# Moving three modulation products of layer 0 from the long convolutions to the filter stage

## The chip, the cores and the metric

The kernel runs on one core of a Trainium2 chip, in one launch. The metric is the device time of that launch in microseconds (us). The core has five engines with queues of their own, each in order: TensorE (PE; its weight loads are shown as PEld), VectorE (DVE), ScalarE (ACT), GpSimd (POOL) and SyncE (SP). In this kernel POOL and SP do little but issue DMA transfers.

## The reference

Two layers of a hybrid block over 512 latent and 256 context tokens of width 1024, in float32. Each layer modulates its input, mixes tokens in four head groups, projects, and runs an MLP:

```python
mod = jax.nn.silu(c) @ w_mod[i] + b_mod[i]          # and mod_c from c_ctx
sh1, sc1, g1, sh2, sc2, g2 = jnp.split(mod[:, None, :], 6, axis=-1)
h = rms_norm(x, norm_mix_pre[i]) * (1.0 + sc1) + sh1
y = token_mixers(h, ...)       # SSD scan, Hyena long convolution, two attentions; then w_out
x = x + g1 * rms_norm(y, norm_mix_post[i])
h = rms_norm(x, norm_mlp_pre[i]) * (1.0 + sc2) + sh2
x = x + g2 * rms_norm(squared_relu_mlp(h, mlp_w1[i], mlp_w2[i]), norm_mlp_post[i])
```

The context tokens go the same way with `mod_c` (in layer 0 only to the end). `w_mod[i]` is 1024 x 6144, so each of the six pieces sh1 to g2 needs a 1024 x 1024 block of it, 4 MB, for two rows of input. The Hyena convolution needs a filter for each layer and sequence length, made by a small network and turned into spectra. The filters depend on weights alone, and the modulation on `c`, `c_ctx` and weights.

## The kernel before

Everything is written in one Python class that emits instructions; a tile framework then sets each engine's order with a scheduler of its own, from the order of the program, priorities and the pools. Weight products are made of three float32r matmuls each (high x high, high x low, low x high; lines 298 to 300).

**The beginning** (`run`). Filter spectra for layer 0's 512 tokens are woven with the first two modulation products (`mod_cols(0, 0, 0)` and `mod_cols(0, 1, 1)`). Then follow `pre_pair` (normalized, modulated and transposed input, tile `xl`/`xc`), the loads of the first two units of `w_in`, and the remaining filters by themselves: layer 1's for 512 tokens and layer 0's for 256 (`filter_seq`). Right after it `qkv_in(0, "d")` makes queries, keys and values of the dense attention; the scheduler lays its 288 matmuls (tile `pg`, 24 for each of six token tiles in q, 24 in kv) between those of the filters. Each filter piece ends in a tile `fk`, of which there is one buffer, written by DVE (lines 721, 722) and sent to the DRAM tensor `spec` by POOL (line 725). There are 12 such pieces after the weave. When the filters are done, their pools are released and attention takes the space.

**A modulation product** is `mod_section` (line 439). It has 8 steps; in each, SP loads a 512 KB piece of `w_mod` into a tile (line 447), and four matmuls of 2 x 256 outputs (line 449) add to four quarters of one PSUM bank. ACT copies the result out (line 457). `mod_cols` then turns the row into columns with 8 transposes (line 510) and a DVE operation or two; `mod_gate` adds `b_mod`, multiplies by a norm weight (line 528) and sends the rows to DRAM (line 530, tile `gated`). Outside the first weave the `w_mod` pieces go into the pool `raw` (tile `r`), three buffers, which the loads of `w_in`, `w_out` and the MLP weights use too (line 354).

**The stage of the long convolutions** (`layer`). After attention and the projections for Hyena and SSD, `weave` interleaves four generators: Hyena for 512 tokens, Hyena for 256 tokens, SSD, and the list `mods`. In layer 0 this list has four modulation products: the gate `g1`, the shift `sh2` and the scale `sc2` of layer 0, and the first of layer 1. Hyena fetches its transform tables (tile `ht`, by POOL) and its spectra (tiles `hf` and `t`, from `spec`, by SP at line 816). Then come `w_out` (tile `py`), the gated norm and the MLP. Layer 1 has the same stage without Hyena for 256 tokens, with four SSD tiles rather than six, and with no modulation product.

The fourth piece of `mod_list(0)`, the gate `g2`, is made in layer 0's MLP in both kernels.

Of the kernel before, what the change touches and what calls it, by code (L numbers as in the profile page):

```python
# [22 lines left out]
SEQ = 512  # L23
CTX = 256
# [141 lines left out]
ME = (4, 1, 2)  # L166
# [7 lines left out]
def chain(*gens):  # L174
    for g in gens:
        yield from g
# [7 lines left out]
class K:  # L184
# [471 lines left out]
    def filter_seq(self, l, n, tabs, v=""):  # L656
        self.mark("filter_seq")
        nc, A = self.nc, self.A
        self.st = "f"
        big = n == SEQ  # L660
        off = 0 if big else SEQ
        h = n // 2
        nj = 2 if big else 1
        nb = 2 * nj
        rl = slice(64 * l, 64 * l + 64)
        for o in range(2):
            ss = self.sm(4, F32, "ss")
            kds = []
            for c in range(2):
                kd = []  # L670
                dec = self.a("dec")[:, :n]
                with self.tc.high_priority(offset=PRIO_W):
                    nc.sync.dma_start(dec, A["decay"][c][:, off:off + n])
                for d in range(2):
                    p = self.a("pf1")[:, :n]
                    ch = 4 * o + 2 * d + c
                    nc.tensor.matmul(p, self.w3[rl, 128 * ch:128 * ch + 128], self.h2[rl, off:off + n], start=True, stop=True)
                    t = self.a("kd" + v)[:, :n]
                    nc.vector.scalar_tensor_tensor(t, p, self.pp[l][:, P_B3 + ch:P_B3 + ch + 1], dec, ADD, MUL)
                    nc.scalar.activation(p, t, AF.Square, accum_out=ss[:, 2 * d + c:2 * d + c + 1])  # L680
                    kd.append(t)
                    yield
                kds.append(kd)
            ms = self.sm(2, F32, "ms", 4)
            nc.vector.scalar_tensor_tensor(ms, ss[:, 0:2], EPS, ss[:, 2:4], ADD, ADD)
            r = self.rsqrt(ms, 2)
            yield
            for c in range(2):
                nc.vector.memset(kds[c][1][:, 0:1], 0.0)
                nc.scalar.activation(kds[c][1], kds[c][1], AF.Copy, scale=r[:, c:c + 1])  # L690
            for cs in range(2):
                X = [self.a("fx" + v, (nb, 256)) for _ in range(2)]
                for c in range(2):
                    kd = kds[c]
                    src = self.a("ko" + v)[:, :n]
                    nc.vector.scalar_tensor_tensor(src, kd[0], r[:, c:c + 1], kd[1], MUL, SUB if cs else ADD)
                    p = self.a("pf2")
                    for par in range(2):
                        for jc in range(nj):
                            s = src[:, 256 * jc + par:256 * jc + 256:2]  # L700
                            b = par * nj + jc
                            nc.tensor.transpose(p[:, 128 * b:128 * b + 128], s, self.ident)
                    pv = p[:, :128 * nb].rearrange("p (b c) -> p b c", c=128)
                    self.hi(X[0][:, :, 128 * c:128 * c + 128], pv)
                    self.lo(X[1][:, :, 128 * c:128 * c + 128], pv, X[0][:, :, 128 * c:128 * c + 128])
                    yield
                for kc in range(h // 128):
                    p = self.a("pmod" if not v and kc % 2 else "pf3")
                    for par in range(2):
                        for jc in range(nj):  # L710
                            b = par * nj + jc
                            if big:
                                th, tl = (tabs[2 * cs + par][:, jc, q, 128 * kc:128 * kc + 128] for q in range(2))
                            else:
                                th, tl = (tabs[0][:, cs, par, q, :] for q in range(2))
                            self.mm3(p[:, 256 * par:256 * par + 256], th, tl,
                                     X[0][:, b, :], X[1][:, b, :], jc == 0, jc == nj - 1)
                    od = self.t2((128, 256))
                    kt = self.a("fk" + v, (2, 256))
                    nc.scalar.activation(od, p[:, 256:512], AF.Copy)  # L720
                    nc.vector.tensor_tensor(kt[:, 0, :], p[:, 0:256], od, ADD)
                    nc.vector.tensor_tensor(kt[:, 1, :], p[:, 0:256], od, SUB)
                    for half in range(2):
                        dst = self.spec[l, n][kc + half * (h // 128)][:, 512 * cs + 256 * o:512 * cs + 256 * o + 256]
                        nc.gpsimd.dma_start(dst, kt[:, half, :])  # L725
                    yield
# [607 lines left out]
    def run(self):  # L1334
        nc = self.nc
        self.plan()
        self.setup()
        pf = self.push("fil", {"fh": (768, F32, 2), "fw": (256, F32, 1),
                               "kd": (512, F32, 4), "ko": (512, F32, 2),
                               "fk": (512, F32, 1), "fw3": (1024, F32, 1), "dec": (512, F32, 2),  # L1340
                               "ft": (1024, F32R, 4), "fx": (1024, F32R, 3)}, "right")
        pp = self.push("pp", {"pf1": (512, F32, 2), "pf2": (512, F32, 2), "pf3": (512, F32, 1),
                              "pmod": (512, F32, 1), "pg": (512, F32, 2)}, psum=True)
        fl = self.push("filL", {"kd0": (512, F32, 8), "ko0": (512, F32, 4), "fk0": (512, F32, 2), "fx0": (1024, F32R, 4), "wm": (1024, F32, 6)})
        self.filter_loads()
        tb = self.filter_tables(SEQ)
        self.filter_head()

        def pre(pair):
            self.mark("pre")  # L1350
            x2 = self.wsp_p.tile([128, 2, 4 * WU], F32, tag="w", name=self.nm("w"))
            xr2 = [x2[:, i, 0:1024] for i in range(2)]
            for i in range(2):
                nc.sync.dma_start(xr2[i], self.x_in(0, 2 * pair + i))
            self.pre_norm(xr2, xr2)
            return xr2
        xr = [pre(0)]
        self.weave((chain(self.mod_cols(0, 0, 0), self.mod_cols(0, 1, 1, P_NMIX)), W0[0]),
                   (self.filter_seq(0, SEQ, tb, "0"), W0[1]))
        self.pop(fl)  # L1360
        XTp = self.push_xt()
        fa = self.push("qkv", self.QKV_TAGS)
        XT = self.new_xt()
        xr += [pre(1), pre(2)]
        for pair in range(3):
            self.mark("pre")
            self.pre_pair(xr[pair], pair, XT, self.mods[0, 1], self.mods[0, 0], EN[0])
        self.load_units(1, 0)
        if self.nl > 1:
            self.do(self.filter_seq(1, SEQ, tb))  # L1370
        self.do(self.filter_seq(0, CTX, self.filter_tables(CTX)))
        self.setup2()
        self.qkv = self.qkv_in(0, "d", XT)
        self.pop(pp)
        self.pop(pf)
        for l in range(self.nl):
            XT, XTp, fa = self.layer(l, XT, XTp, fa)

    def layer(self, l, XT, XTp, fa):
        nc = self.nc  # L1380
# [3 lines left out]
        more = l + 1 < self.nl  # L1384
# [27 lines left out]
        YT = self.new_xt((0,), need)  # L1412
        self.load_units(self.upos[l, "o", 3])
        hys = [(self.hyena(l, SEQ, 0, YT), W2[0])]
        mods = self.mod_list(l)[0 if l == 0 else ME[0]:3 if l == 0 and more else 9]
        if need:
            hys.append((self.hyena(l, CTX, SEQ, YT), W2[3]))
        if l + 1 < self.nl:
# [215 lines left out]
```

## Time and profile before

| | before |
|---|---|
| median of 3 runs (range) | 1924.27 us (1921.92 to 1924.78) |
| the profiled execution | 1919.0 us |
| its span, first to last instruction | 1917.2 us |
| PE / DVE / ACT / POOL busy | 93% / 68% / 44% / 5% of the span |
| mean granted TensorE clock | 0.974 of full speed |
| chain that ended last, by engine | PE 76%, DVE 9%, issue 6%, DMA 4%, ACT 4% |
| DMA | 235 MB, mean 123 GB/s |

The profile shows one execution. Busy time of PE is modelled (matmuls are pipelined, and their ends are worked out), so a share of 95% does not mean that PE issues without a gap; the spacing of the starts tells that. The share of DMA is that of 16 engines; the clock is the mean that was granted, where 1.00 is 2.4 GHz.

### The profile page before, as it was taken

How to read it: one execution, taken by the hardware profiler on the slowest of the kernel's cores; microseconds unless marked ns; L12 is line 12 of the kernel's file. 1: busy time of each engine (PE TensorE's matmuls, PEld its weight loads, DVE VectorE, ACT ScalarE, POOL GpSimd, SP SyncE). 2: the span in 40 equal slices, each digit the busy share in tenths (PEclk: the TensorE clock that was granted, in tenths of full speed). 3: DMA queues.
4: the chain of work that ended last, by engine and by line, in shares of the span. 5: the costliest groups of instructions: out<-in, count | busy, mean ns of one | idle time of the engine just before them, and what ended most of it. 6: DMA issues, size and time to landing. Idle time of an engine off the chain costs nothing.

```text
span 1917.2 us, 27370 instructions
## 1 busy us (share of the span) xinstructions
PE 1790.2 (93%) x10170; PEld 1482.7 (77%) x10170; DVE 1297.7 (68%) x2897; ACT 836.8 (44%) x1804; POOL 91.5 (5%) x176
## 2 busy tenths in 40 slices
PE   6899999978879999999999998899978789999998
PEld 2688888845668888888888888888866688888886
DVE  4878888877756656676666658988878563444446
ACT  4844565536515532322222327556546263332322
POOL 0120001011000000000000000000010000000000
PEclk9999999989989999999999999999989899999999
DMA  8531121278833244333333415112183243233232
GB/s 291 187 111 53 39 74 58 69 260 272 290 107 132 93 135 136 121 107 114 121 121 121 142 47 176 45 48 89 45 273 120 74 157 113 91 99 99 88 102 85
DMA packets 137597, 235.16 MB, mean 123 GB/s; under 512 B 12466, under 2 KB 77395, under 8 KB 137464
## 3 DMA queue, kind: packets, MB, share of 16 engines
q1 hardware_dynamic: 122920, 186.12, 30.2%
q0 software_dynamic: 14544, 47.30, 7.1%
q8 instruction: 80, 1.31, 0.3%
q14 instruction: 53, 0.43, 0.1%
HBM read 206.74 MB, written 26.64 MB: 122 GB/s over the span
## 4 chain that ended last, share of the span: by engine, by line
PE 76%; DVE 9%; issue 6%; DMA 4%; ACT 4%; POOL 1%; SPq 0%; DVEq 0%; ACTq 0%; POOLq 0%
PE pg L298 19%; PE pg L299 18%; PE pg L300 18%; PE po L1294 3%; PE py L298 2%; PE py L299 2%; PE pm L1286 2%; PE py L300 2%; PE ps L1249 1%; PE ps L1250 1%; PE pm L1206 1%; PE psd L1052 1%; DMA spec<-fk 1%; POOL spec L725 1%; DMA r<-in_w_mod_dram 1%
## 5 line engine op out<-in xcount | busy, mean ns | idle before, releaser
L265 ACT ACTIVATE w<-r 128x1024 fp32r<-128x1024 f32 (+1 forms) x176 | 186.6, 1061 | 348.1 <-PE pg L300 325.1
L270 DVE TENSOR_TENSOR w<-r,w 128x1024 fp32r<-128x1024 f32 (+1 forms) x176 | 214.1, 1223 | 106.1 <-ACT w L265 105.2
L298 PE MATMUL pg<-xl,w 128*128 128x512 f32 (+1 forms) x704 | 269.5, 386 | 2.2 <-DVE ya L1311 0.9
L300 PE MATMUL pg<-xl,w 128*128 128x512 f32 (+1 forms) x704 | 269.7, 384 | 0.0
L299 PE MATMUL pg<-xl,w 128*128 128x512 f32 (+1 forms) x704 | 269.7, 384 | 0.0
L298 PE MATMUL pg<-w,H 128*128 128x512 f32 x640 | 250.1, 391 | 0.0
L299 PE MATMUL pg<-w,H 128*128 128x512 f32 x640 | 249.2, 390 | 0.0
L300 PE MATMUL pg<-w,H 128*128 128x512 f32 x640 | 249.0, 389 | 0.0
L476 DVE SCALAR_TENSOR_TENSOR x<-r,scT,x 128x512 f32<-128x512 f32 x168 | 119.1, 746 | 71.7 <-DMA r<-in_w_mod_dram 71.7
L298 PEld LDWEIGHTS pg<-xl,w 128*128 128x128 f32 x704 | 132.6, 190 | 27.7 <-issue 2.2
L300 PEld LDWEIGHTS pg<-xl,w 128*128 128x128 f32 x704 | 133.3, 189 | 22.9
L299 PEld LDWEIGHTS pg<-xl,w 128*128 128x128 f32 x704 | 133.3, 189 | 22.2 <-DVE xl L270 0.2
L298 PEld LDWEIGHTS pg<-w,H 128*128 128x128 f32 x640 | 120.1, 188 | 26.8 <-issue 1.7
L300 PEld LDWEIGHTS pg<-w,H 128*128 128x128 f32 x640 | 120.1, 188 | 25.0
L299 PEld LDWEIGHTS pg<-w,H 128*128 128x128 f32 x640 | 120.2, 188 | 24.4
L1520 ACT ACTIVATE t<-pg 128x512 f32<-128x512 f32 (+1 forms) x100 | 50.4, 506 | 198.0 <-PE pg L300 198.0
L1551 DVE TENSOR_TENSOR ya<-pg,ya 128x512 f32<-128x512 f32 x120 | 81.8, 687 | 69.0 <-PE pg L300 68.7
L1522 DVE TENSOR_TENSOR t<-t 128x512 f32<-128x512 f32 (+1 forms) x100 | 58.1, 582 | 83.7 <-ACT H L1521 83.6
L300 PE MATMUL pg<-xc,w 128*128 128x256 f32 (+1 forms) x368 | 104.4, 284 | 0.0
L298 PE MATMUL pg<-xc,w 128*128 128x256 f32 (+1 forms) x368 | 103.3, 284 | 1.1 <-ACT xc L265 1.1
L299 PE MATMUL pg<-xc,w 128*128 128x256 f32 (+1 forms) x368 | 104.1, 284 | 0.0
L298 PE MATMUL pg<-w,xl 128*128 128x256 f32 (+1 forms) x320 | 93.0, 292 | 5.4 <-ACT qk L1113 2.5
(357 smaller groups left out, 3866.1 us busy)
## 6 DMA issues: line engine op xcount, KB each, us to landing
r<-in_mlp_w_dram SPq DMA_DIRECT2D x128, 512.0 KB
r<-in_w_mod_dram SPq DMA_DIRECT2D x80, 512.0 KB
r<-in_w_in_dram SPq DMA_DIRECT2D x40, 512.0 KB
ht<-in_inv_dram POOLq DMA_DIRECT2D x20, 512.0 KB, 5.4
ht<-in_fwd_dram POOLq DMA_DIRECT2D x18, 512.0 KB, 5.4
wm<-in_w_mod_dram SPq DMA_DIRECT2D x16, 512.0 KB
r<-in_w_out_dram SPq DMA_DIRECT2D x16, 512.0 KB
xd<-x POOLq DMA_DIRECT2D x16, 512.0 KB, 3.3
```

Of the source, the lines that this page charges most:

```text
L265: self.nc.scalar.activation(dst, src, AF.Copy)
L270: self.nc.vector.tensor_tensor(dst, src, h.bitcast(F32), SUB)
L298: mm(out, ah, bh, start=first, stop=False)
L299: mm(out, ah, bl, start=False, stop=False)
L300: mm(out, al, bh, start=False, stop=last)
L476: nc.vector.scalar_tensor_tensor(acc[:, c], raw[:, k], sc, acc[:, c], MUL, ADD)
L725: nc.gpsimd.dma_start(dst, kt[:, half, :])
L1286: nc.tensor.transpose(p[:, n:n + 128], P[:, col:col + 128], self.ident)
L1294: nc.tensor.matmul(po[:, qo:qo + m], V[:, c, :], pt[:, hl, cols[j]:cols[j] + m], start=i + j == 0 and hl == 0, stop=i + j == len(kts) - 1 ...
L1520: nc.scalar.activation(r, p[:, :nn], AF.Relu)
L1522: nc.vector.tensor_tensor(r, r, r, MUL)
L1551: nc.vector.tensor_tensor(dst, p, dst, ADD)
```

## The change

The three products `g1`, `sh2` and `sc2` of layer 0 leave the stage of the long convolutions and are woven with the remaining filters of the beginning, one step of theirs for two of the filters'. They take the PSUM bank `pmod`, which every second filter matmul group used till now; that one now uses `pf2`, whose two buffers the filters' transposes use as well. The list `mods` of layer 0 keeps one product, the first of layer 1.

```diff
                 for kc in range(h // 128):
-                    p = self.a("pmod" if not v and kc % 2 else "pf3")
+                    p = self.a("pf2" if not v and kc % 2 else "pf3")
...
         self.load_units(1, 0)
-        if self.nl > 1:
-            self.do(self.filter_seq(1, SEQ, tb))
-        self.do(self.filter_seq(0, CTX, self.filter_tables(CTX)))
+        self.weave((self.filters_rest(tb), 2), (chain(*self.mod_list(0)[:3 if self.nl > 1 else 4]), 1))
         self.setup2()
...
+    def filters_rest(self, tb):
+        if self.nl > 1:
+            yield from self.filter_seq(1, SEQ, tb)
+        yield from self.filter_seq(0, CTX, self.filter_tables(CTX))
...
-        mods = self.mod_list(l)[0 if l == 0 else ME[0]:3 if l == 0 and more else 9]
+        mods = [] if l == 0 else self.mod_list(l)[ME[0]:]
         if need:
             hys.append((self.hyena(l, CTX, SEQ, YT), W2[3]))
         if l + 1 < self.nl:
             mods += self.mod_first(l + 1)[:ME[1]]
```

How the scheduler's order moves is seen at three places.

**PE, at the end of the filters.** `pf` is a filter product, `pg` one of the dense attention's projection (with `w_918` and `w_923` for the queries, `w_928` and `w_933` for keys and values), `pmod` a modulation product. Before, around the last filter product:

```order
L299 MATMUL pg_1723<-w_933,xl_157_691 128x256
L299 MATMUL pf_379_1473<-fx_1458,ft_1271 128x256
L300 MATMUL pf_379_1473<-fx_1457,ft_1271 128x256
L298 MATMUL pf_379_1473<-fx_1457,ft_1271 128x256
L299 MATMUL pf_379_1473<-fx_1458,ft_1271 128x256
L300 MATMUL pf_379_1473<-fx_1457,ft_1271 128x256
L300 MATMUL pg_1723<-w_933,xl_173_707 128x256
```

With the change, around the same product:

```order
L298 MATMUL pg_1830<-w_918,xc_150_684 128x256
L299 MATMUL pf_414_1640<-fx_1618,ft_1366 128x256
L300 MATMUL pf_414_1640<-fx_1618,ft_1366 128x256
L298 MATMUL pf_414_1640<-fx_1618,ft_1366 128x256
L299 MATMUL pf_414_1640<-fx_1619,ft_1366 128x256
L300 MATMUL pf_414_1640<-fx_1618,ft_1366 128x256
L299 MATMUL pg_1830<-w_918,xc_150_684 128x256
L449 MATMUL pmod_1524<-r_1666,scT 2x256 x4
L300 MATMUL pg_1830<-w_918,xc_166_700 128x256
```

Before, 215 of the 288 projection matmuls stand ahead of the last filter matmul; with the change 130 do, with the 24 modulation steps (96 matmuls of line 449) among them, the first of which stands among the transposes of `pre_pair` (line 593).

**SP, in the filter stage.** With the change, the first `w_mod` loads follow the decay table of the short filter, and the loads of the next `w_in` unit (`r_1856`) stand behind all 24:

```order
L673 DMA dec_1369<-in_decay_dram 128x256
L447 DMA r_952<-in_w_mod_dram 128x1024
L447 DMA r_970<-in_w_mod_dram 128x1024
L447 DMA r_1009<-in_w_mod_dram 128x1024
...
L447 DMA r_1654<-in_w_mod_dram 128x1024
L447 DMA r_1660<-in_w_mod_dram 128x1024
L447 DMA r_1666<-in_w_mod_dram 128x1024
L354 DMA r_1856<-in_w_in_dram 128x4x256
```

Before, the `w_in` loads follow `dec` directly, and the three other decay tables of the short filter come among them; now these stand behind the 8th, the 12th and the 15th of the `w_mod` loads.

**SP, late in the stage of the long convolutions.** `hf` are the spectra of the second convolution of the 512 tokens. Before:

```order
L816 DMA hf_6314<-spec_512_111 128x2x256
L447 DMA r_6353<-in_w_mod_dram 128x1024
L447 DMA r_6385<-in_w_mod_dram 128x1024
L1072 DMA sz_6136<-sz_107 128x256
L1072 DMA sz_6220<-sz_107 128x256
L447 DMA r_6391<-in_w_mod_dram 128x1024
L447 DMA r_6423<-in_w_mod_dram 128x1024
L354 DMA r_6598<-in_w_out_dram 128x2x512
L816 DMA hf_6359<-spec_512_111 128x2x256
```

With the change:

```order
L1440 DMA t_6564<-yy_109 128x256
L1440 DMA t_6568<-yy_109 128x512
L1440 DMA t_6572<-yy_109 128x256
L1440 DMA t_6576<-yy_109 128x512
L816 DMA hf_6361<-spec_512_111 128x2x256
L816 DMA hf_6394<-spec_512_111 128x2x256
L1072 DMA sz_6232<-sz_107 128x256
L1072 DMA sz_6304<-sz_107 128x256
L816 DMA hf_6420<-spec_512_111 128x2x256
```

No `w_mod` load stands between the spectra any more (the 8 that are left come at the head of the stage); five loads of attention results (`t`, for `w_out`) now stand ahead of three of the spectra.

## Rows read from the trace of the kernel before

**Rows 1.** Busy time by stretch: columns PE, PEld, DVE, ACT, POOL, clock, DMA share, GB/s.
```profile
core 0: us, PE busy (x) PEld busy (x) DVE busy (x) ACT busy (x) POOL busy (x), PEclk, DMA share, GB/s
425.00:543.00 118.00, 96.53 (x679) 66.69 (x679) 82.86 (x210) 61.80 (x192) 9.55 (x18) 0.88 0.75 254
460.00:500.00 40.00, 37.72 (x304) 25.34 (x303) 32.79 (x83) 27.84 (x91) 2.30 (x5) 1.00 0.75 243
...
1430.00:1499.00 69.00, 51.55 (x334) 39.89 (x333) 59.08 (x141) 42.11 (x126) 4.24 (x8) 0.95 0.41 131
```

**Rows 2.** The same view of the filter stage of the beginning.
```profile
40.00:70.00 30.00, 27.21 (x189) 17.70 (x189) 23.54 (x90) 20.42 (x43) 6.47 (x12) 1.00 0.90 311
96.00:146.00 50.00, 47.45 (x348) 43.93 (x347) 35.23 (x114) 22.52 (x64) 12.82 (x24) 0.97 0.35 109
...
83.00:153.00 70.00, 63.92 (x464) 57.55 (x462) 52.11 (x161) 38.39 (x99) 13.45 (x25) 0.98 0.29 90
```

**Rows 3.** Chain that ended last, 425 to 543 us, shares by line.
```profile
by line: DMA r<-in_w_mod_dram 9.2%; PE pg L449 8.5%; DMA hf<-spec 8.5%; PE psd L1052 8.2%; DMA ht<-in_inv_dram 6.2%; DMA t<-us 4.3%; PE psd L1043 4.1%; DMA gated<-t 3.7%; issue 3.4%; PE ph L298 3.2%; PE pc L298 3.1%; PE ps L1063 3.0%; DVE w
```

**Rows 4.** Line 449 alone, 425 to 543 us: PE and PEld busy.
```profile
425.00:543.00 118.00, 20.29 (x208) 3.90 (x208) 0.88 0.75 254
```

**Rows 5.** SP's waits, 395 to 545 us: line, waited for, total, times, longest.
```profile
SPq L447 <- PE pg L449: 42.3, 19, 6.8
SPq L354 <- DVE wx L270: 15.1, 2, 14.4
```

**Rows 6.** SP in order of time, late in that stage: start, duration, instruction.
```profile
486.76 10.27 SPq L447 DMA_DIRECT2D r<-in_w_mod_dram  x4
497.12 0.53 SPq L816 DMA_DIRECT2D hf<-spec  x1
...
509.17 0.54 SPq L816 DMA_DIRECT2D hf<-spec  x1
```

**Rows 7.** PE in order of time, one transposition and three modulation steps.
```profile
494.90 0.65 PE L510 MATMUL pg<-ident,t 2*128 2x2 f32 x8
...
496.03 1.69 PE L449 MATMUL pg<-r,scT 128*2 128x256 f32 x24
497.86 0.35 PE L298 MATMUL ph<-hx,ht 128*128 128x256 f32 x1
```

**Rows 8.** PE in order of time, two projection matmuls at full rate.
```profile
95.42 0.28 PE L299 MATMUL pg<-w,xl 128*128 128x256 f32 x1
95.54 0.28 PE L300 MATMUL pg<-w,xl 128*128 128x256 f32 x1
```

**Rows 9.** DVE in order of time: `fk` pieces under load and after, first and last.
```profile
46.31 0.42 DVE L721 TENSOR_TENSOR fk<-pf,t 128x256 f32<-128x256 f32 x1
...
51.48 0.42 DVE L721 TENSOR_TENSOR fk<-pf,t 128x256 f32<-128x256 f32 x1
...
56.54 0.42 DVE L721 TENSOR_TENSOR fk<-pf,t 128x256 f32<-128x256 f32 x1
...
75.49 0.41 DVE L721 TENSOR_TENSOR fk<-pf,t 128x256 f32<-128x256 f32 x1
...
95.51 0.42 DVE L721 TENSOR_TENSOR fk<-pf,t 128x256 f32<-128x256 f32 x1
...
144.83 0.43 DVE L721 TENSOR_TENSOR fk<-pf,t 128x256 f32<-128x256 f32 x1
```

**Rows 10.** The `spec` writes of line 725: time to landing.
```profile
DMA to landing us min/median/max: 2.0/2.1/6.8
```

**Rows 11.** DVE in order of time after the filters: last pieces before the attention's norms.
```profile
151.86 1.23 DVE L270 TENSOR_TENSOR w<-r,w 128x1024 fp32r<-128x1024 f32 x1 [0.68 <-ACT w L265]
...
154.57 0.54 DVE L1144 TENSOR_REDUCE dss<-tP 128x6 f32<-128x384 f32 x1
...
158.10 1.03 DVE L1161 TENSOR_TENSOR qk<-qk,drr 128x384 f32<-128x384 f32 x2
```

**Rows 12.** DVE's part of the modulation, line 528, 425 to 543 us.
```profile
425.00:543.00 118.00, 2.62 (x4) 0.88 0.75 254
```

## The prediction

> **What bounds the kernel now.** I read the busy time by stretch first, for the two stages that the change touches. In the stage of the long convolutions, from 425 us to its end at 543 us, no engine is full [rows 1]: DVE is busy 82.86 of 118 us (0.70), PE 96.5 by a model that flatters it, and DMA runs at 0.75 with a clock of 0.88 on average between its levels of 1.2 and 2.4 GHz. The reader is to see the contrast in the same rows: the middle of the stage, 460 to 500 us, has DVE at 0.82, and layer 1's stage, which has no modulation product in it, has DVE at 0.86 for all of its 69 us, with DMA at 0.41. So something other than DVE's work makes layer 0's stage long.
>
> The chain of waits names it. Of those 118 us, 9.2% wait for a `w_mod` load, 8.5% are the modulation's matmuls, 3.7% wait for the write of a gate (its tile holds a buffer that a load of Hyena wants) and 8.5% wait for spectra [rows 3]. SP's waits say why the spectra are late: SP is one queue, and its `w_mod` loads (line 447) stand there for 42.3 us in all until PE gives a `raw` buffer back [rows 5]. From 486.8 us four of them take SP 10.27 us, and the next spectrum is issued behind them; a later one only at 509 us [rows 6]. The stage is bound by waits among queues, of which the modulation is the largest.
>
> The filter stage looks different. From 96 to 146 us PE shows 47.45 of 50 us, DMA only 0.35 [rows 2]. But the records there say that PE is not full: two projection matmuls at full rate start 0.12 us apart [rows 8], so the 464 records between 83 and 153 us [rows 2] would need 464 x 0.12 = 56 us of 70. What paces the filters is the single `fk` buffer: the 12 pieces after the weave's end follow each other from 95.5 to 144.8 us [rows 9], (144.83 - 95.51) / 11 = 4.5 us each with pauses, while a write lands 2.1 us after its issue [rows 10] and DVE and POOL have their part around it.
>
> **The gain: what the long convolutions lose.** 24 of 26 modulation steps in the 118 us go (208 records of line 449, 8 to a step), PE busy 24/26 x 20.29 = 18.7 us [rows 4], and 24 x 512 KB = 12.6 MB of loads. On DVE little goes: 2.62 us of the gate's rows [rows 12] and two small additions. The chain bounds the gain from above: 9.2% + 3.7% of 118 us, and 24/26 of the 8.5%, is 10.9 + 4.4 + 9.3 = 24.6 us, if nothing else is late behind it. From below I take only the waits for `w_mod`, 10.9 us. Between them I go by DVE, whose work stays: 82.9 - 2.6 = 80 us. At 0.86, layer 1's share, it takes 93 us (25 us less); at 0.82, the share of this stage's own dense part, 98 us, **20 us less**. I take the second, since here two more SSD tiles and the short Hyena run on the same buffers, and since the product that is left loads at the head of the stage, where nothing changes. What is late next is DVE itself and the SSD chain. The order bears this out only in so far as the spectra no longer stand behind `w_mod` loads; five loads of attention results now stand ahead of three of them and may hold them in their turn, which is one more reason not to take 25.
>
> The clock adds nothing of its own: its dips there come with PE's waits, and are inside the 0.88 of those rows.
>
> **The cost: what the filter stage gets.** PE: three steps take from 496.03 us to the next matmul at 497.86 us, 0.61 us each, and eight transposes 0.65 us [rows 7]; 24 x 0.61 + 2 x 0.65 = 15.9 us, all of it in a stage where PE has holes. How much falls on the path is read from the order. Attention's norms (`dss`, line 1144) need all 288 projection matmuls; before, they end at 155 us, ten after the last `fk` [rows 9, 11]. Before, 215 of them stand ahead of the last filter matmul, so 73 x 0.12 = 8.8 us are left behind it. With the change 130 stand ahead, 158 x 0.12 = 19.0 us are left, and the last step and transposes (1.3 us) too. So even if the filters end at the same moment, attention begins 19.0 + 1.3 - 8.8 = **11.5 us later**: the scheduler put the modulation where the projection was. There is one refund: the split of the next `w_in` unit on DVE stands at 151.9 us just ahead of the last `dss` [rows 11], two such of 1.23 us. It now comes earlier in the projection's tail, and I count half, 1 us.
>
> The filters' own end is the unknown. The `fk` loop now shares the DMA engines with 12.6 MB in some 60 us, 210 GB/s on top of about 109 GB/s [rows 2], less the `w_in` loads that now follow. The trace has this case: from 46 to 75 us, at a share of 0.90 and 311 GB/s [rows 2], eight pieces follow each other in (75.49 - 46.31) / 7 = 4.2 us, though the first two gaps are 5.2 and 5.1 us [rows 9]. So between 0 (the mean, no slower than later) and 12 x 1.0 = 12 us (all at the slow gap against 4.2); PE's waits for `w_mod` in a queue that also holds the filters are inside this, as three buffers and a pace of some 2.5 us a step (24 in 60 us) leave them little. I take 3 us, near the mean of the loaded stretch. The bank moved from `pmod` to `pf2` I cost at nothing: `fk` paces these products, and the bank of one is free long before `fk` is. **Sum: 11.5 - 1 + 3 = 13.5 us**, from 9 to 24.
>
> By the Trainium skill's page "DMA: Bandwidth & Descriptors" (section "Issuing engines are not separate DMA queues"), transfers started by SP and by POOL run on the same 16 DMA engines and interleave. That speaks against this change, since `spec` writes and `w_mod` loads would slow each other; by it alone the upper end of 12 us would stand and the sum be 22.5 us. The loaded rows show some of it (two slow gaps) and not the rest.
>
> Nothing later pays: the rows of the gate and the two column products are used only in `w_out` and the MLP, and attention between the stages moves as a whole.
>
> **Sum.** 13.5 - 20 = -6.5 us. The profiled execution took 1919.0 us and the median is 1924.27, 5.3 us above it, so I carry the difference over: 1924.3 - 6.5 = 1917.8, say **1918 us**. A measurement of this kernel tells 0.2%, 3.8 us, from no change.
>
> **The rivals.**
>
> *The filters wait for the DMA engines* (slower). The `fk` loop runs at the slow gap, 1 us more for each of 12 pieces, and PE's queue stalls on `w_mod` tiles, so the cost is 11.5 - 1 + 12 = 22.5 us or more; and the gain is that of the chain's lower part, 11 to 16 us. 22.5 - 14 = +8.5, **1933 us**. It decides from some 0.6 us more per piece on, with the gain at 14. For it: the two gaps of 5.2 us, one `spec` write of 6.8 us [rows 10], three decay tables that now queue behind `w_mod` loads. Against: after those two the five gaps at the same load are 3.8 us on average, (75.49 - 56.54) / 5 [rows 9].
>
> *The stage of the long convolutions is as tight as its SSD chain* (no change). The gain is the 10.9 us of `w_mod` waits, or somewhat over; spectra still come late, now behind the attention results in SP's queue. 13.5 - 12 = +1.5: **1926 us**. For it: the dense 40 us at 0.82 [rows 1] have modulation in them and hardly suffer. Against: layer 1's 0.86.
>
> *PE's holes take the modulation* (much faster). The 14 us that 464 records leave free of 70 take nearly all 15.9 us, cost 2 to 4, gain 25: -22, **1902 us**. Against it stands the order at the end of the filters, which is fixed; only filters that end some 8 us sooner could bring it, and their `fk` loop doesn't allow that.
>
> That the change doesn't do what it says is ruled out by the order: the 24 steps do stand there.
>
> **How the numbers follow.** My forecast, a gain of 4 to 17 us, gets 0.45; the slower rival 0.23, no change 0.25, much faster 0.07. That makes faster 0.52, same 0.25, slower 0.23. The forecast's own range is 1907 to 1920. The range for 8 in 10 leaves out most of the much faster case and the far end of the slower one: from 9 - 25 = -16 and a little of the last rival, 1906, to 24 - 12 = +12, 1936.
>
> **What would show it.** Right: `dss` ends some 13 us after 155; from there the attention is the same; the first `py` comes some 6 us before 543 us; DVE's share in the stage is near 0.82 and line 816 no longer stands behind line 447. Wrong on the cost: the spacing of line 721 over 5 us, or PE idle before line 449 by DMA. Wrong on the gain: DVE's share stays at 0.7 and line 816 waits behind line 1440.

## The result and the profile after

| | before | after |
|---|---|---|
| median of 4 runs each, taken side by side (range) | 1923.1 us (1921.58 to 1924.78) | 1945.82 us (1943.07 to 1947.4) |
| span of the profiled execution | 1917.2 us | 1942.8 us |
| mean granted TensorE clock | 0.974 | 0.969 |

The changed kernel is slower: 1.0116 of the time before, interval 1.0099 to 1.0134, some 23 us. The prediction was 1918 us, faster, with a range up to 1936 us, so the time lies outside it.

The first thing to do with two traces is to follow a few landmarks that both have. They come from the views in order of time, in us from the start of the span:

| landmark | before | after | later by |
|---|---|---|---|
| last `fk` piece (DVE, line 721) | 144.83 | 169.50 | 24.7 |
| last `dss` of the dense attention (line 1144) | 154.57 | 189.72 | 35.2 |
| stage of the long convolutions: first load of `hz` (line 774) | 393.05 | 426.68 | 33.6 |
| its first SSD triangle product (line 1043) | 457.12 | 491.63 | 34.5 |
| its last copy of a convolution (ACT, line 857) | 532.11 | 557.24 | 25.1 |
| end of the span | 1917.2 | 1942.8 | 25.6 |

So 35.2 us are lost by the first attention. Of these 1.5 come back before the stage of the long convolutions begins, 0.9 more are lost up to its first triangle product, and 9.4 come back between that product and the end of the convolutions. The parts of the stage on either side of that product are called the head and the second half below.

**The loss.** DVE in order of time after the change, line 721, the pieces that answer to [rows 9]; the bracket says how long DVE was idle and what ended it:

```profile
98.35 0.41 DVE L721 TENSOR_TENSOR fk<-pf,t 128x256 f32<-128x256 f32 x1
...
105.98 0.42 DVE L721 TENSOR_TENSOR fk<-pf,t 128x256 f32<-128x256 f32 x1 [4.09 <-DMA spec<-fk]
...
111.97 0.42 DVE L721 TENSOR_TENSOR fk<-pf,t 128x256 f32<-128x256 f32 x1 [3.00 <-DMA spec<-fk]
...
144.40 0.42 DVE L721 TENSOR_TENSOR fk<-pf,t 128x256 f32<-128x256 f32 x1 [4.19 <-DMA spec<-fk]
...
169.50 0.42 DVE L721 TENSOR_TENSOR fk<-pf,t 128x256 f32<-128x256 f32 x1 [4.95 <-DMA spec<-fk]
```

Twelve pieces again, at (169.50 - 98.35) / 11 = 6.5 us each where [rows 9] gave 4.5. DVE's waits say what it stands for; what makes that long is tested below. First the wait in the changed kernel (76 to 180 us: total, times, longest), then its landing times of all `spec` writes, which answer to [rows 10]:

```profile
DVE fk L721 <- DMA spec<-fk: 22.3, 7, 5.0
...
DMA to landing us min/median/max: 2.1/4.3/7.6
```

The same two lines of the kernel before:

```profile
DVE fk L721 <- DMA spec<-fk: 3.6, 3, 2.7
...
DMA to landing us min/median/max: 2.0/2.1/6.8
```

The writes of this stretch alone have the same medians, 2.1 us before (95 to 146 us) and 4.3 after (98 to 171 us). The remaining filters have one `fk` buffer, so a piece can't be written until the last has landed. By that, a write that takes 4.3 us in place of 2.1 would lengthen the cycle by some 2.2 us. The waits grew by 22.3 - 3.6 = 18.7 us, most of the 11 x 2.0 = 22 us by which the row of pieces grew.

**The stage of the long convolutions**, by halves (PE, PEld, DVE, ACT, POOL, clock, DMA share, GB/s). Before:

```profile
393.05:457.12 64.07, 47.64 (x325) 30.38 (x325) 43.45 (x97) 24.73 (x69) 10.29 (x20) 0.81 0.93 309
457.12:532.11 74.99, 68.55 (x495) 48.09 (x494) 53.62 (x130) 45.14 (x142) 4.77 (x9) 0.93 0.77 261
```

After:

```profile
426.68:491.63 64.95, 43.87 (x289) 30.57 (x289) 41.49 (x94) 24.69 (x69) 9.20 (x18) 0.82 0.87 284
491.63:557.24 65.61, 55.07 (x324) 44.24 (x322) 52.44 (x125) 40.48 (x128) 4.88 (x9) 0.92 0.43 126
```

The second half went from 75.0 to 65.6 us, and DVE's share in it from 0.72 to 0.80. The head did not move: DMA is at 0.93 and 0.87 there, and DVE at 0.68 and 0.64. Its DMA traffic, by the view of the transfers in those stretches:

```profile
DMA packets 9154, 19.80 MB, mean 309 GB/s; under 512 B 964, under 2 KB 4932, under 8 KB 9150
...
r<-in_w_mod_dram SPq DMA_DIRECT2D x15, 512.0 KB
...
ht<-in_fwd_dram POOLq DMA_DIRECT2D x6, 512.0 KB, 5.8
```

and after:

```profile
DMA packets 9537, 18.43 MB, mean 284 GB/s; under 512 B 887, under 2 KB 5239, under 8 KB 9533
...
r<-in_w_mod_dram SPq DMA_DIRECT2D x7, 512.0 KB
ht<-in_inv_dram POOLq DMA_DIRECT2D x7, 512.0 KB, 6.4
ht<-in_fwd_dram POOLq DMA_DIRECT2D x6, 512.0 KB, 5.6
r<-in_w_out_dram SPq DMA_DIRECT2D x3, 512.0 KB
...
hf<-us SPq DMA_DIRECT2D x2, 256.0 KB
```

Of the 24 `w_mod` loads that left the stage, eight left the head (15 to 7), 4.2 MB, and the others the second half. Three `w_out` loads and two loads of the convolution's own data (`us`) came forward into the head; the spectra are as many as before. It carries 1.4 MB less and takes 0.9 us more, so its bytes alone don't set its length.

### The profile page after: what moved, and what is told of

Its sections match the earlier page's. It is cut to its first block, busy times and chain, and to the rows that moved or that the text cites. A ratio compares the mean times of both kernels' runs of the same rounds, so it can differ in the third digit from the quotient of the medians.

```text
span 1942.8 us, 27360 instructions
## 1 busy us (share of the span) xinstructions
PE 1801.0 (93%) x10170; PEld 1486.8 (77%) x10170; DVE 1298.5 (67%) x2897; ACT 836.7 (43%) x1804; POOL 91.4 (5%) x176
## 4 chain that ended last, share of the span: by engine, by line
PE 77%; DVE 8%; issue 6%; DMA 4%; ACT 4%; POOL 1%; SPq 0%; DVEq 0%; ACTq 0%; POOLq 0%
PE pg L298 19%; PE pg L299 19%; PE pg L300 19%; PE po L1294 3%; PE pm L1286 2%; PE py L298 2%; PE py L299 2%; PE py L300 2%; PE ps L1249 1%; DMA ht<-in_inv_dram 1%; DMA spec<-fk 1%; PE pmod L449 1%; PE ps L1250 1%; PE pm L1206 1%; PE pf L677 1%
```

## The experiments

Edits are against the changed kernel unless said otherwise. A kernel with a line added has the later lines numbered one higher. A time with an interval is the median of several runs, and its ratio is to the kernel before beside them; the others are one execution. The kernel before took 1920 to 1922 us beside these runs (medians), and 1926.11 us in its one execution beside the last three.

**Is it the loads or the matmuls that slow the filters?** Two runs take one half of the modulation away, within the filter stage only. In the first, only the first of a product's 8 pieces is loaded, and all 8 steps use it:

```diff
-            raw = ...
-            nc.sync.dma_start(raw, ...)
+            if k == 0 or "wm" in self.slots or "fk" not in self.slots:
+                raw = ...
+                nc.sync.dma_start(raw, ...)
```

> The changed kernel; in the filter stage each of the three products loads only its first w_mod piece and uses it in all 8 steps (so these three products are left out in effect; PE's work is the same). Theory A: spec writes land in 2 to 2.5 us again, gaps between pieces 4 to 4.7 us, last piece at 145 to 152 us, attention begins 20 us sooner than in the changed kernel, about 1926 us. Theory B: last piece at 163 us or later, 1940 us or more.

In the second all pieces are loaded, and only the first is multiplied:

```diff
+            one = "fk" in self.slots and "wm" not in self.slots
-            for q in range(4):
+            for q in range(4 if k == 0 or not one else 0):
...
-                                 raw[:, 256 * q:256 * q + 256], start=k == 0, stop=k == 7)
+                                 raw[:, 256 * q:256 * q + 256], start=k == 0, stop=one or k == 7)
```

> The changed kernel; in the filter stage all w_mod pieces are loaded but only the first of each product's 8 steps is multiplied (7 of 8 left out of the sum). Theory A: with the loads there, spec writes still land in some 4 us, the gaps stay at 5.5 to 6.5 us, last piece at 158 us or later. Theory B: the pieces come at 4 to 4.7 us, last one by 150 us.

Measured: 1920.88 us without the loads, 1943.9 us with the loads alone. The same two lines of the first (steps, no loads):

```profile
DVE fk L722 <- DMA spec<-fk: 4.2, 4, 2.2
...
DMA to landing us min/median/max: 2.0/2.5/7.1
```

and of the second (loads, no steps):

```profile
DVE fk L722 <- DMA spec<-fk: 22.2, 9, 5.4
...
DMA to landing us min/median/max: 2.0/4.3/7.5
```

The loads make nearly the whole loss of the filters. Without them the last `fk` comes at 146.41 us, 1.6 after that of the kernel before, and the last `dss` at 166.59, 12.0 later than before: that is the part of the order. With them and no matmuls the last `fk` comes at 172.15. That is 2.7 us later than with the matmuls, at a granted clock of 0.82 in place of 0.91, so the second run bears the loads out, but doesn't measure them by itself. PE waits for a `w_mod` load only three times in the changed kernel, 1.9 us in all (76 to 180 us).

**Is the single `fk` buffer the place where it hurts?** Every second piece gets another buffer:

```diff
-                    kt = self.a("fk" + v, (2, 256))
+                    self.alt = not v and not getattr(self, "alt", False)
+                    kt = self.t2((128, 2, 256)) if self.alt else self.a("fk" + v, (2, 256))
```

> The changed kernel, every second piece of the remaining filters written into a tile of the common pool (t) instead of the single buffer fk. Theory A (the w_mod loads lengthen the landing of the spec writes from 2.1 to 4.3 us, and through the one fk buffer every piece waits for it): the pieces of line 721 no longer wait for spec, the last one comes at 145 to 155 us instead of 169.5, and the kernel takes 15 to 20 us less than the changed one, 1926 to 1931 us. Theory B (PE's queue: the modulation steps stand ahead of the filter products, and the pieces come late whatever the buffer): the last piece stays at 163 us or later, the time within 5 us of 1946.

> The kernel before with the same second buffer. Theory A: there the writes land in 2.1 us and the loop of 4.1 to 4.5 us is only partly on the path, so 0 to 6 us less than before (1917 to 1923). Theory B: no change, within 2 us.

Measured: in the changed kernel 1934.63 us, ratio to before 1.0077 (1.0049 to 1.0105), against 1.0116. The last `dss` comes at 175.79 us, 13.9 sooner, and 12.9 of these are left at the first output of attention (257.7 to 244.8 us). In the kernel before the same edit gives 0.9985 (0.9964 to 1.0006), no difference. The writes land no sooner (median 4.9 us), but DVE has no wait for them any more: most of what the loads cost comes by the one buffer, which puts the landing on the path. Not all of it. The last piece comes at 153.62 us, 15.9 sooner than in the changed kernel, but still 7.2 later than without the loads (8.8 later than before). There PE waits 4.7 us for `w_mod` loads, and DVE 8.9 us for ACT's copy of a piece (76 to 180 us); no run takes these apart. The piece came within the range of theory A; the time, 1926 to 1931 us by it, did not, and the five runs lie far apart (1930.28 to 1946.65 us), so the trace carries this reading more than the ratio.

**Does the moved PSUM bank cost anything?** The kernel before, with that line of the change alone:

```diff
-                    p = self.a("pmod" if not v and kc % 2 else "pf3")
+                    p = self.a("pf2" if not v and kc % 2 else "pf3")
```

> The kernel before, with the changed kernel's PSUM bank (pf2 in place of pmod) and nothing else. The bank is free long before the fk buffer is, so all theories expect no change: within 2 us of before. A rival (the bank is part of the filters' longer way): 3 us or more slower.

Measured: 0.9994 (0.9977 to 1.0012). In the kernel before it costs nothing.

**Why did the second stage give so little back?** SP's queue after the change shows two long stops ahead of spectra (start, duration):

```profile
456.36 12.41 SPq L354 DMA_DIRECT2D r<-in_w_out_dram  x3
468.88 0.54 SPq L816 DMA_DIRECT2D hf<-spec  x1
...
513.50 13.29 SPq L1440 DMA_DIRECT2D t<-yy  x5
526.83 1.19 SPq L816 DMA_DIRECT2D hf<-spec  x2
```

The second is the new wait that the prediction had feared; the first it did not name. One run lets the `w_out` loads come late, by a low priority:

```diff
-        self.load_units(self.upos[key] + ahead)
+        self.load_units(self.upos[key] + ahead, 200 if key[0] == 0 and key[1] == "o" else PRIO_W)
```

> The changed kernel, with the three w_out loads that stand ahead of a spectrum in SP's queue (12.4 us there, waiting for raw buffers that the last modulation product holds) put later. Theory C (SP's queue: w_out's loads took the place of w_mod's ahead of the spectra, and hold the convolution): the spectrum of the third block comes at about 456 us instead of 469, the first convolution ends 6 to 12 us sooner, the kernel takes 1934 to 1940 us. Theory D (the stage is bound by the transform tables, 22 loads through three ht buffers): within 3 us of 1946.

Another gives the attention results a buffer of a later pool, which takes them out of the way of the spectra:

```diff
-                y_ = self.t2()[:, :nn]
+                y_ = (self.a("x", (512,)) if l == 0 else self.t2())[:, :nn]
```

> The changed kernel, with the eight loads of attention results for w_out into tiles of a pool that is there only after the convolutions, so that none stands ahead of a spectrum in SP's queue. Theory E (five of these loads hold the last three spectra for 15 us, and the second convolution with them): spectra of the second convolution follow within 8 us of each other, the convolutions end 5 to 10 us sooner; w_out then waits some 4 us for these loads, so 1937 to 1944 us. If they hold nothing (DVE and the SSD chain bound that part): the convolutions end within 2 us of the same, and the time is 1946 to 1950 us.

Measured: 1939.93 us, 1.0096 (1.0062 to 1.013), with the `w_out` loads late; the spectrum is issued 10 us sooner (458.63 in place of 468.88 us), and the stage is 1.3 us shorter. The interval overlaps that of the changed kernel, so the time by itself shows no gain. With the results later 1954.79 us, 1.019 (1.0159 to 1.0221): from the end of the convolutions to the first gated pair it takes 57.8 us where the changed kernel takes 41.5. The first stop therefore does not bound the stage. The second could not be taken away. With the results out of the way two spectra stop all the same:

```profile
510.60 13.19 SPq L816 DMA_DIRECT2D hf<-spec  x2
```

The view of SP's waits puts 12.4 us of this on DVE's work on `sy` (line 1070), and the stage is only 3.2 us shorter (127.4 against 130.6). So theories C and E, which took the stops for the stage's bound, don't fit these stages (the time with the `w_out` loads late is at the edge of C's range): the length of a stop in a queue is not its price.

Combinations: two `fk` buffers with late `w_out` loads, and the results later as a third.

> The changed kernel with the second buffer for fk and with w_out's loads late. If theories A and C are each right and add up: 1934.6 less 6 to 12 us, 1923 to 1929 us, so no better than before. If C is wrong: 1932 to 1936 us.

> The changed kernel with a second fk buffer, w_out loads late and the attention results later. By theories A, C and E 1920 to 1926 us; if E is wrong 1930 to 1934 us.

Measured: 1930.25 us, 1.0043 (1.0026 to 1.006), the best of the changed kernel and still slower than before; 1946.82 us, 1.0136 (1.0117 to 1.0156), with the third, where neither range of its expectation was met.

Then the product that is left in the stage, the first of layer 1, was sent to the MLP, in the changed kernel and in the one before:

```diff
-ME = (4, 1, 2)
+ME = (4, 0, 2)
```

> The changed kernel, with the last modulation product too taken out of the convolutions' stage (made in the MLP with the other of layer 1). Theory F (the head of the stage, 64 us from the first load of Hyena to the first SSD decay product in both kernels, is set by the contention with the one product that is left there): 64 falls to 55 or less, and the convolutions end 8 us sooner or more; the MLP pays up to 5 us, 1936 to 1943 us. If the head is the chain of DRAM round trips and table loads: 62 us or more stay, and the time is within 4 us of 1946.

> The kernel before, with the product of layer 1 moved from the convolutions' stage to the MLP (three products left there). Theory F says 5 to 10 us less in that stage; less whatever the MLP pays, so 1915 to 1921 us. If the queues' waits do not add up but stand beside another chain: within 4 us of before, or slower by what the MLP pays.

Measured: 1947.29 us, 1.0146 (1.0119 to 1.0173); and 1926.42 us, 1.0032 (1.002 to 1.0044). The halves of the changed kernel without the product:

```profile
422.72:475.13 52.41, 33.47 (x206) 26.94 (x206) 41.12 (x93) 23.26 (x65) 9.20 (x18) 0.80 0.86 260
475.13:547.78 72.65, 56.46 (x334) 44.96 (x333) 52.50 (x125) 40.62 (x129) 4.75 (x9) 0.93 0.42 123
```

The head falls from 65.0 to 52.4 us, as theory F said, but the second half grows from 65.6 to 72.7, and what is left of the gain is lost behind the stage: by the profiled execution, the fastest of four, the stage ends 9.5 us sooner and the span is 3.4 us shorter. In the kernel before, the stage stays at 139.8 us, as with the product (139.1), where theory F wanted 5 to 10 less.

**What bounds the head?** One 512-token convolution reads four forward and four inverse tables. These runs load one of each and use it throughout, first in the second convolution, then in the first, then in both, last in both with the product in the MLP. The edit for the first convolution (the others differ in the condition):

```diff
-                i = kc if big else 0
+                i = kc if big and not (l == 0 and not o) else 0
...
-                tb = self.a("ht")
-                nc.gpsimd.dma_start(tb, A["inv%d" % n][kc])
+                if kc == 0 or not (big and l == 0 and not o):
+                    tb = self.a("ht")
+                    nc.gpsimd.dma_start(tb, A["inv%d" % n][kc])
```

> The changed kernel; in layer 0's second convolution of the 512 tokens one forward and one inverse table are loaded and used four times each (a wrong transform, the same matmuls, 6 of 22 table loads fewer). Theory D: the second convolution, 39 us from its first table to its last, takes 25 us or less, and the kernel some 10 to 15 us less, 1931 to 1936 us. Theory C: little in this part, within 4 us of 1946.

> The changed kernel, in which the first of the two 512-token convolutions of layer 0 loads one forward and one inverse transform table and uses it in all its steps (so its values are not the reference's); six loads of 512 KB, 3.1 MB, leave the head of the long-convolution stage, whose 65 us move 18.5 MB at a DMA share of 0.88. Theory A, the head is bound by the table loads: the time from the load of hz to the first SSD triangle product falls from 64.9 us by 8 to 11, and the end of the stage comes some 8 us sooner, span 1932 to 1936. Theory B, the hand-offs of SSD and of the second convolution after the head bound the stage: the head may shorten, but the last hf<-ph copy comes under 4 us sooner, span 1939 to 1943.

> The changed kernel, in which both 512-token convolutions of layer 0 load one forward and one inverse table each and use it throughout (values not the reference's). If the tables bound the stage in both halves, it falls below what the first convolution's alone gives, by 5 us or more; if only the head is bound by them, both give the same within 2 us.

> As the run with all tables once, and the modulation product that is left goes to the MLP: what stays of the stage is Hyena, SSD and their hand-offs with little DMA. It gives the floor of the stage. Theory A: under 115 us from the load of hz to the last hf<-ph copy (130.6 in the changed kernel, 139 before). Theory B: 122 or more.

Measured: the second convolution's tables change nothing (1943.35 us, span 1941.6, the stage 131.3 us). The first's take 11.4 us off the span (1933.22 us, span 1931.4), and the end of the convolutions comes 11.0 us sooner. Its halves:

```profile
424.44:481.02 56.58, 42.63 (x295) 29.54 (x295) 40.24 (x90) 24.04 (x67) 6.04 (x12) 0.82 0.84 272
481.02:546.29 65.27, 51.87 (x318) 41.29 (x317) 53.33 (x130) 41.12 (x131) 4.75 (x9) 0.97 0.45 125
```

Both convolutions' tables (1933.13 us, no less than with the first's alone), and the same with no product (1943.62 us; the stage takes 114.6 us, as its theory A said, but 13.3 us more pass behind it):

```profile
427.02:480.94 53.92, 40.48 (x294) 27.53 (x293) 39.80 (x88) 23.56 (x66) 6.43 (x13) 0.87 0.89 285
480.94:545.76 64.82, 52.91 (x317) 40.79 (x317) 53.52 (x132) 41.50 (x133) 1.20 (x3) 0.97 0.26 78
```

```profile
428.40:478.88 50.48, 34.35 (x230) 28.32 (x229) 41.70 (x96) 23.37 (x66) 6.57 (x13) 0.83 0.74 232
478.88:542.98 64.10, 52.12 (x294) 39.24 (x294) 51.94 (x123) 39.97 (x128) 1.06 (x2) 0.93 0.24 71
```

So the table loads hold the head: 15.39 MB in place of 18.43 make it 8.4 us shorter, with 1.3 us less on DVE and 0.7 on ACT. Whether it is their bytes, at a DMA share of 0.84 to 0.93, or the waits for single loads was not taken apart. The second half stays between 64.1 and 65.6 us at DMA shares of 0.43, 0.45, 0.26 and 0.24. So with the three products gone its transfers don't bound it any more, and DVE is at 0.80 to 0.83. That this is DVE with the hand-offs of SSD and Hyena around it is argued from the share; no run shows which hand-off it is. The one exception, the 72.7 us of the run without a product and with all tables, falls to 64.1 when the tables go too, so there they held it.

## Why the prediction was wrong, point by point

- **The term for the filters' end ("I take 3 us", from 0 to 12) failed most.** It measured 24.7 us: 2.8 in the start of the first piece and 21.8 over the eleven gaps. The loads are the cause (23.1 of it go with them). Its place and half of its mechanism stood in the slower rival: the writes were late, but PE's queue hardly stood for `w_mod` tiles (1.9 us). Its size there, 1 us for each piece, was half of what came. Its sign in the prediction, a spacing of line 721 over 5 us, came true with 6.5.
- **The step that failed in it** was to take the spacing of the loaded stretch from 46 to 75 us for the price of contention [rows 2, 9]. There the writes land in 4.0 us by the median, and still the pieces follow at 4.2 us. The two lines are the wait that ends in a landing (total, times) and the landing times, in the kernel before from 45 to 76 us:

```profile
  DVE fk L721: 0.4, 1
...
DMA to landing us min/median/max: 2.1/4.0/6.8
```

The kernel before says why that stretch is another case. Its pieces are those of the first weave, which come from the tag `fk0` with two buffers; the remaining filters use `fk` with one (the third number, lines 1340 and 1344):

```python
                               "fk": (512, F32, 1), "fw3": (1024, F32, 1), "dec": (512, F32, 2),
...
        fl = self.push("filL", {"kd0": (512, F32, 8), "ko0": (512, F32, 4), "fk0": (512, F32, 2), "fx0": (1024, F32R, 4), "wm": (1024, F32, 6)})
```

So "one buffer" holds for the remaining filters only, and the prediction read the price of a loop with one buffer from a loop with two. The run with two buffers fits this: its writes land in 5.1 us (98 to 160 us), and DVE has no wait for them. The first weave with one buffer was not run, and its other tiles have more buffers too. The sum that the trace did support is the cycle of one buffer: 4.5 us with 2.1 us of landing in it, so 4.5 + 4.0 - 2.1 = 6.4 us with the landing of the loaded stretch, against 6.5 measured. That it comes so near is in part luck, since the second buffer takes back 15.9 of the 24.7 us and not all.
- By the Trainium skill's page "DMA: Bandwidth & Descriptors" (section "Issuing engines are not separate DMA queues") the writes and the loads interleave on the same engines. The landing of 2.1 to 4.3 us agrees. The 12 us that the prediction set beside this rule were a price from the loaded rows, and too small.
- **The order term held.** 11.5 - 1 = 10.5 us were expected from the projection's matmuls behind the filters. From the last `fk` to the last `dss` it is 20.2 us after and 9.7 before, 10.5 more. The refund of 1 us came too, though not as described: two splits of the `w_in` unit still stand just ahead of the last `dss` (187.00 and 188.45 us), but PE, which waits 1.1 us for DVE there before, shows no wait there after.
- **The bank at nothing held** (0.9994), and so did "nothing later pays", within 0.5 us: 25.1 us at the end of the convolutions, 25.6 at the end of the span.
- **The gain of 20 us failed: it was 8.5**, or 9.4 in the second half less 0.9 in the head. The step was "at 0.82, the share of this stage's own dense part", put on all of the stage. It is right for the second half, which came to 0.80, and wrong for the head, which came to 0.64 and is held by its loads at a DMA share of 0.87 to 0.93; [rows 1] gave one mean over both, 0.75. The chain's `w_mod` share [rows 3] was read as time to be had, but a third of the loads lay in the head, and others came forward there. The signs "DVE's share stays at 0.7" (0.70 before, 0.72 after, over both halves) and "line 816 waits behind line 1440" both came true; but line 1440 is not what holds the spectra, as they stop as long with its loads out of the way.
- The sum with the measured sizes: 24.7 + 10.5 = 35.2 lost; 35.2 - 1.5 until the stage begins, less 8.5, is 25.2 us at its end, against 25.1 read from the trace.

The range was too narrow by 10 us because both terms of its bad end, a cost of 24 and a gain of 12, were set by the same two mistakes.

## What to carry to other kernels

Loads that are moved beside a loop with a single buffer can lengthen every turn of it: add the change of the landing time, read from a stretch with the new load, to each turn, or give the loop a second buffer first. Before the pace of one stretch is taken as the price for another, compare how many buffers the two have. Before a stage's average share is made into a gain, cut the stage where its DMA share changes; the head, which its loads hold, gave nothing back here, since other loads came forward into the room. Moved loads should be priced in the place where they arrive, even where that place shows a DMA share of only 0.35.

## What was not expected of the hardware

At a DMA share of 0.69 on average (98 to 171 us, 221 GB/s) the median landing of a 128 KB write doubled, 2.1 to 4.3 us. And the granted clock went with PE's busy time. From 96 to 172 us, before, after, with the steps and no loads, and with the loads and no steps (PE first, the clock third from the end):

```profile
96.00:172.00 76.00, 70.09 (x528) 66.07 (x526) 57.53 (x179) 32.41 (x94) 13.45 (x25) 0.97 0.29 89
96.00:172.00 76.00, 67.36 (x496) 46.02 (x495) 39.33 (x122) 27.38 (x73) 14.47 (x27) 0.91 0.70 225
96.00:172.00 76.00, 75.16 (x630) 64.19 (x629) 49.44 (x156) 33.82 (x96) 14.53 (x27) 1.00 0.37 109
96.00:172.00 76.00, 60.10 (x370) 51.87 (x370) 41.59 (x129) 29.82 (x81) 13.45 (x25) 0.82 0.71 224
```

These are means of a stretch; the clock has two levels, 1.00 (2.4 GHz) and half of it.
